# Moving half a gate's projection ahead of the attention output's projections, and respreading the work behind them

## The chip, the cores and the metric

The kernel runs on one core of a Trainium2 chip. The metric is the device time of one execution in microseconds (us); smaller is better. Every engine of the core (TensorE for products, VectorE, ScalarE and GpSimd for elementwise work, SyncE for issuing DMAs) runs its own list of instructions in order and waits for others through semaphores. The order within each list is fixed when the program is built: a planner goes through the program in its written order, estimates when each instruction's operands and buffers are ready, and gives an engine that is free the earliest-written instruction that is ready by that estimate.

## The reference

One encoder block over 512 tokens of width 1024, in float32:

```
z  = rmsnorm(x) @ W_in                 # a_q a_k a_v a_z, b_q b_k b_v, i_q i_k i_w, gate_a, gate_b
oA = gated_delta_rule(conv(a_q, a_k, a_v), ...) * silu(a_z)      # chunks of 64 tokens, 8 heads
oB = attention(rope(b_q), rope(b_k), b_v; 128 keys per query chosen by the indexer i_q, i_k, i_w)
x  = x + (sigmoid(gate_a) * (oA @ W_a) + sigmoid(gate_b) * (oB @ W_b)) @ W_out
x  = x + moe(rmsnorm(x))               # 16 experts, two per token
```

The delta rule solves, for each chunk and head, a unit lower triangular system of 64 x 64. The kernel inverts its diagonal blocks of 32 x 32 and combines them by products.

## The kernel before

**Pieces of weights.** A float32 product is done as three products of a high and a low half. The weights arrive in pieces of 256 rows by up to 512 columns, listed in `plan` by `want(key, ...)`. For each piece SyncE loads `raw` (three buffers), ScalarE copies the high half `whi`, and VectorE or GpSimd subtracts to get the low half `wlo` (two buffers each); the last argument of `want` names the engine of the low half. TensorE then runs 24 products on a piece. `tok_gen` and `feat_gen` are generators that yield after each piece; what stands between two yields is written behind the piece. A projection holds four accumulation banks and evacuates them after its last piece. Three more banks, `pm`, serve everything else.

**Order of the projections before:** "kv", "iq", "bq", "qk0", "v", "qk1", "gb0", "gb1" (the second gate), then "pb" (the attention output by W_b, two chunks of two pieces), "ga0", "z", "ga1" (the first gate in two halves, with "z" between), then the solve and "pa". "ga" is spilled to memory by `gate_spill` (four DMAs of 256 KB for each half).

**Behind the pieces.** `behind_projections()` yields once for each of the 24 pieces of "bq", "qk0", "v", "qk1", "gb0", "gb1" and takes that many steps of three generators: `PICKS` of `choose()` (the indexer's scores and the 128 largest of each row, 62 steps, VectorE's `max` and `match_replace`), `LOOKS` of `attention()` (53 steps), `NORMS` of `norms`. What is left over is drained behind "gb0" (choice) and "gb1" (attention). The query tiles of indexer and attention share the tag `tokq` with four buffers.

**The delta rule's systems.** `pre(g)`, for each of two groups of heads, has two steps for each of four token tiles: the first makes the system's matrices `ke` (products `pg`, `pkk`; exponentials; four products on VectorE) and writes the diagonal blocks to memory (`lane_n`, four DMAs); the second transposes keys and values and scales them (`r`, `kd` on VectorE, `qd` and a mask over `ke` on GpSimd). `pre(0)` runs behind the pieces of "pb", `pre(1)` behind three pieces of "ga0". `lanes()` then loads all diagonal blocks with one block on each partition (`LN`) and inverts them by a recurrence of 31 multiplies and 31 reductions on VectorE, each needing the one before. Its result `X` goes to memory (`lane_x`) and comes back as `TT`, with which `solve` begins. "z" and "ga1" are TensorE's work beside the recurrence.

Of the kernel before, what the change touches and what calls it, by code (L numbers as in the profile page):

```python
# [7 lines left out]
F32 = mybir.dt.float32  # L8
# [10 lines left out]
T = 4  # L19
# [12 lines left out]
LOWS_A = "DDDPDDPD"  # L32
PICKS = (0, 1, 5, 4, 5, 6, 0, 6, 4, 4, 5, 3, 5, 0, 4, 5, 4, 3, 2, 7, 0, 0, 0, 0)
LOOKS = (0, 0, 0, 0, 0, 0, 0, 0, 1, 2, 0, 4, 1, 2, 6, 3, 7, 2, 5, 6, 4, 6, 6, 0)
NORMS = (0, 0, 0, 0, 0, 0, 0, 0, 0, 1, 1, 1, 1, 1, 1, 0, 0, 2, 1, 1, 1, 1, 2, 2)
# [64 lines left out]
def body(tc, x, positions, norm1_g, w_in, w_proj_a, w_proj_b, w_out, norm2_g,  # L100
# [130 lines left out]
    for hf in range(2):  # L231
        want(f"gb{hf}", win, 8, [(GATE_B + 512 * hf, 512)], *low(LOWS[24 + 4 * hf:28 + 4 * hf]))
    for hf in range(2):
        want(f"pb{hf}", w_proj_b[0], 4, [(512 * hf, 512)], DVE)
    want("ga0", win, 8, [(GATE_A, 512)], *low(LOWS_A[:4]))
    want("z", win, 8, [(A_Z, 456)], POOL)
    want("ga1", win, 8, [(GATE_A + 512, 512)], *low(LOWS_A[4:]))
# [267 lines left out]
    def ev_iq(t, acc):  # L505
        q = AT_([128, 8, 64], name=f"iq{t}", tag="tokq", bufs=4)
# [137 lines left out]
    def ev_w3(t, acc):  # L644
        q = AT_([128, 8, 64], name=f"bq{t}", tag="tokq", bufs=4)
# [181 lines left out]
    for _ in gate_gen(1):  # L827
        tick(bg)
# [40 lines left out]
    def pre(g):  # L869

        Q = groups[g]
        hs = slice(4 * g, 4 * g + 4)
        Q.gl = []
        for t in range(T):
# [4 lines left out]
            eg = GP([128, 2, 128], name="eg", tag="eg", bufs=2)  # L879
# [22 lines left out]
            for b in range(4):  # L902
                SP.dma_start(lanes_of(lane_n, t, g, b), ke[32 * b:32 * b + 32, :, 0, 32 * b:32 * b + 32])
            yield
            ps = bank()
# [11 lines left out]
            Q.gl.append(gl)  # L917
            yield

    def lanes():  # L920

        LN = Ft([L, 32, 32], F32, "LN", "v0")
        SP.dma_start(LN, lane_n)
        X = Ft([L, 32, 32], F32, "X", "v1")
        POOL.memset(X, 0.0)
        POOL.memset(X.rearrange("p a b -> p (a b)")[:, ::33], 1.0)
        tmp = Ft([L, 1024], F32, "ltmp", "kq3")
# [7 lines left out]
        for d in range(1, 32):  # L935
# [3 lines left out]
            DVE.tensor_reduce(skew(flat[0], d, n, 1, 1), tv, axis=AX.X, op=OP.add)  # L939
# [144 lines left out]
    def z_chunk():  # L1084
        def ev(t, acc):
# [7 lines left out]
            zv = z.rearrange("p (h d) -> p h d", h=8)  # L1093
            POOL.tensor_tensor(zv, zv, angh[:, None, :].to_broadcast([128, 8, 64]), op=OP.mult)
# [13 lines left out]
    pre0, pre1 = pre(0), pre(1)  # L1108
    for hf in range(2):
        for _ in proj_b(hf):  # L1110
            tick([(pre0, 2)])
    drain(pre0)
    rk1 = [Ft([128, 2, 1024], F32, f"rk1{i}", ("obh", "obl")[i]) for i in range(2)]
    place(1, [ke_[1][:, t] for t in range(T)], [rk1[t // 2][:, t % 2] for t in range(T)])
    ga0 = gate_spill(0)
    for _ in range(3):
        tick([(ga0, 1), (pre1, 3)])
    drain(pre1)
    for t in range(2):
        clear_TT(t)  # L1120
    X = lanes()
# [670 lines left out]
```

## Time and profile before

| | |
|---|---|
| time, median of 3 runs | 724.35 us (723.95 to 725.03) |
| profiled execution: time, span | 722.27 us, 720.1 us |
| TensorE products, busy | 660.6 us (92%) |
| VectorE, busy | 531.5 us (74%) |
| ScalarE, busy | 412.9 us (57%) |
| GpSimd, busy | 258.9 us (36%) |
| chain that ended last | TensorE 61%, VectorE 22%, GpSimd 5% |

The span is the time between the profiled execution's first and last instruction; its own time is 2.2 us longer. Products are pipelined: a product's row shows some 0.39 us while the next one starts 0.23 us later, so TensorE's pace is read from starts, not from lengths.

### The profile page before, as it was taken

Reading aid. Unit: us, or ns where it says so; the run is one execution under the profiler, and the core shown is the slowest. Engines: PE = TensorE matmul, PEld = TensorE weight load, DVE = VectorE, ACT = ScalarE, POOL = GpSimd, SP = SyncE. Lnnn points to the kernel's source line nnn. Section 1 sums busy time; section 2 is a strip of 40 time slices with the busy share of each in tenths; the row PEclk is TensorE's granted clock in tenths of the full one; section 3 lists DMA queues with packets and bytes.
Section 4 is the critical chain, followed back from the end, with each engine's and each line's share of the span. In section 5 each row is a group of like instructions: output and inputs, shape, how many; then the busy total and the mean of one; then the engine's idle time right before and its main releaser. Section 6 shows DMA issues by size and latency. Waiting matters only on the chain.

```text
span 720.1 us, 10544 instructions
## 1 busy us (share of the span) xinstructions
PE 660.6 (92%) x3460; PEld 539.8 (75%) x3460; DVE 531.5 (74%) x1130; ACT 412.9 (57%) x736; POOL 258.9 (36%) x268
## 2 busy tenths in 40 slices
PE   3999977889889999999879999899999999999991
PEld 3888756666666777778768998878897888888871
DVE  4572689999995565642994566766678999999885
ACT  5443464586969764343323332344256998999863
POOL 3226716536341222345263111571142342334113
PEclk9999988999999999999999999999999999999996
DMA  7433213113130212325326200979779999999963
GB/s 264 114 108 88 86 30 89 58 31 87 30 88 5 84 58 63 74 57 148 88 76 182 94 2 1 348 235 355 257 235 311 352 294 287 300 276 274 289 213 119
DMA packets 84025, 110.76 MB, mean 154 GB/s; under 512 B 17435, under 2 KB 57883, under 8 KB 83840
## 3 DMA queue, kind: packets, MB, share of 16 engines
q1 hardware_dynamic: 79360, 101.70, 44.2%
q0 software_dynamic: 4320, 7.77, 4.4%
q8 instruction: 28, 0.46, 0.3%
q10 hardware_dynamic: 288, 0.59, 0.2%
q14 instruction: 29, 0.24, 0.1%
HBM read 101.22 MB, written 16.78 MB: 164 GB/s over the span
## 4 chain that ended last, share of the span: by engine, by line
PE 61%; DVE 22%; POOL 5%; issue 4%; DMA 4%; ACT 3%; SPq 0%; POOLq 0%; DVEq 0%; ACTq 0%
PE acc L130 47%; PE pm L130 5%; DVE xh L447 4%; DVE sn L595 3%; DVE ltmp L938 3%; DVE m L594 3%; DVE sn L585 2%; PE pm L1528 2%; POOL wlo L155 1%; DVE X L939 1%; POOL mTl L1209 1%; DMA x<-in_x_dram 1%; PE po L130 1%; ACT whi L154 1%; DMA xe<-h2d,ids 1%
## 5 line engine op out<-in xcount | busy, mean ns | idle before, releaser
L154 ACT ACTIVATE whi<-raw 128x1024 fp32r<-128x1024 f32 (+1 forms) x123 | 127.0, 1049 | 106.2 <-PE acc L130 83.5
L155 DVE TENSOR_TENSOR wlo<-raw,whi 128x1024 fp32r<-128x1024 f32 (+1 forms) x88 | 110.5, 1282 | 36.3 <-ACT whi L154 29.5
L155 POOL TENSOR_TENSOR wlo<-raw,whi 128x1024 fp32r<-128x1024 f32 (+1 forms) x35 | 89.0, 2542 | 124.0 <-ACT whi L154 107.0
L130 PE MATMUL acc<-hTh,whi 128*128 128x512 f32 x224 | 91.9, 410 | 5.1 <-ACT xh L445 4.2
L130 PE MATMUL acc<-hTh,wlo 128*128 128x512 f32 x224 | 90.4, 404 | 6.0 <-DVE wlo L155 5.9
L130 PE MATMUL acc<-whi,xhl 128*128 128x512 f32 x256 | 91.3, 410 | 0.3 <-DVE xhl L1535 0.3
L130 PE MATMUL acc<-hTl,whi 128*128 128x512 f32 x224 | 90.3, 403 | 0.0
L130 PEld LDWEIGHTS acc<-hTh,whi 128*128 128x128 f32 x224 | 43.7, 195 | 18.2 <-ACT xh L445 5.0
L130 PEld LDWEIGHTS acc<-hTh,wlo 128*128 128x128 f32 x224 | 43.5, 194 | 16.6 <-DVE wlo L155 7.3
L130 PEld LDWEIGHTS acc<-whi,xhl 128*128 128x128 f32 x256 | 48.1, 188 | 10.1 <-DVE xhl L1535 0.8
L130 PEld LDWEIGHTS acc<-hTl,whi 128*128 128x128 f32 x224 | 43.5, 194 | 10.1 <-issue 1.7
L130 PE MATMUL acc<-wlo,xhl 128*128 128x512 f32 x128 | 50.4, 394 | 0.0
L130 PE MATMUL acc<-whi,hTh 128*128 128x456 f32 (+1 forms) x120 | 46.1, 388 | 0.0
L1573 POOL DMA_INDIRECT accd<-yb,ids x14 | 23.9, 1704 | 58.7 <-ACT ah L154 58.7
L130 PE MATMUL acc<-wlo,hTh 128*128 128x456 f32 (+1 forms) x120 | 44.9, 374 | 0.0
L130 PE MATMUL acc<-whi,hTl 128*128 128x456 f32 (+1 forms) x120 | 44.7, 372 | 0.0
L1372 POOL DMA_INDIRECT xe<-h2d,ids x15 | 22.5, 1498 | 42.4 <-PE pm L1528 35.7
L447 DVE SCALAR_TENSOR_TENSOR xh<-xrb,sm,xh 128x511 f32<-128x511 f32 (+2 forms) x36 | 30.2, 891 | 0.0
L130 PE MATMUL acc<-whi,mTh 128*128 128x512 f32 (+1 forms) x72 | 27.4, 380 | 1.1 <-DVE ma L1203 1.1
L594 DVE MAX8 m<-sn 128x8 f32<-128x256 f32 (+2 forms) x48 | 26.6, 557 | 2.1 <-POOL sn L587 1.4
L130 PEld LDWEIGHTS acc<-wlo,xhl 128*128 128x128 f32 x128 | 24.2, 189 | 3.7
L938 DVE TENSOR_TENSOR ltmp<-X,LN 128x31 f32<-128x31 f32 (+15 forms) x31 | 20.5, 661 | 8.3 <-DMA LN<-lane_n 7.4
(466 smaller groups left out, 1662.4 us busy)
## 6 DMA issues: line engine op xcount, KB each, us to landing
raw<-in_w_in_dram SPq DMA_DIRECT2D x24, 512.0 KB, 3.6
raw<-in_w_exp_gate_dram SPq DMA_DIRECT2D x42, 256.0 KB, 8.2
raw<-in_w_exp_up_dram SPq DMA_DIRECT2D x42, 256.0 KB, 7.9
raw<-in_w_exp_down_dram SPq DMA_DIRECT2D x21, 512.0 KB, 9.5
raw<-in_w_in_dram SPq DMA_DIRECT2D x16, 256.0 KB, 3.2
raw<-in_w_out_dram SPq DMA_DIRECT2D x8, 512.0 KB, 9.1
raw<-in_w_in_dram SPq DMA_DIRECT2D x8, 456.0 KB, 3.5
x<-in_x_dram SPq DMA_DIRECT2D x4, 512.0 KB, 7.0
```

The costliest lines, as they stand in the source:

```text
L130: return ins_of(PE.matmul(o, l, r, start=start, stop=stop, skip_group_check=True))
L154: h = ins_of(ACT.activation(hi, src, AF.Copy))
L155: return h, ins_of((lo_eng or DVE).tensor_tensor(lo, src, f32(hi), op=OP.subtract))
L447: DVE.scalar_tensor_tensor(xh[:, j:], xr[:, :512 - j], cw[:, blk, 3 - j:4 - j], xh[:, j:], op0=OP.mult, op1=OP.add)
L585: DVE.scalar_tensor_tensor(s, r[:, :N], iwn[:, h:h + 1], s, op0=OP.mult, op1=OP.add)
L594: DVE.max(m8, sn[t])
L595: DVE.match_replace(out=sn[t], in_to_replace=m8, in_values=sn[t], imm_value=-2 * BIG)
L938: DVE.tensor_tensor(tv, skew(flat[0], 0, n, d, 1), skew(flat[1], d, n, d, 32), op=OP.mult)
L939: DVE.tensor_reduce(skew(flat[0], d, n, 1, 1), tv, axis=AX.X, op=OP.add)
L1372: return ins_of(POOL.indirect_dma_start(out=xe, out_offset=None, in_=h2d[0:128 * tiles], in_offset=bass.IndirectOffsetOnAxis(ap=idc, axis= ...
L1528: PE.transpose(ps[:, d * 128:(d + 1) * 128], xe[:, k * 128:(k + 1) * 128], C("ident"))
L1573: return ins_of(POOL.indirect_dma_start(out=accd, out_offset=bass.IndirectOffsetOnAxis(ap=idc, axis=0), in_=y, in_offset=None, bounds_chec ...
```

## The change

- "ga0" is projected and spilled directly after "gb1", ahead of "pb". Choice, attention and norms are spread over 28 pieces ("bq" to "ga0") by new tuples, and attention is drained behind "ga0".
- `pre(g)` is split into `systems(g)` (matrices and `lane_n`) and `sides(g)` (transposes and scales). Behind each of the four pieces of "pb" goes one step of `systems` of both groups; behind each piece of "z" one step of `sides` of both groups.
- `lanes()` is written behind "z"; `LN`, `X` and a smaller scratch have tiles of their own. Only "ga1" is written behind it.
- The low halves of "ga0", "z" and "ga1" are all VectorE's (before: GpSimd had one of "ga0", all of "z", one of "ga1").
- The four multiplications of `z` by the norm's gain on GpSimd are queued behind the recurrence's last instruction.
- `tokq` has six buffers instead of four.

```
-LOWS_A = "DDDPDDPD"
-PICKS = (0, 1, 5, 4, 5, 6, 0, 6, 4, 4, 5, 3, 5, 0, 4, 5, 4, 3, 2, 7, 0, 0, 0, 0)
-LOOKS = (0, 0, 0, 0, 0, 0, 0, 0, 1, 2, 0, 4, 1, 2, 6, 3, 7, 2, 5, 6, 4, 6, 6, 0)
-NORMS = (0, 0, 0, 0, 0, 0, 0, 0, 0, 1, 1, 1, 1, 1, 1, 0, 0, 2, 1, 1, 1, 1, 2, 2)
+PICKS = (0, 2, 3, 4, 4, 4, 3, 3, 3, 3, 3, 3, 3, 3, 3, 3, 3, 3, 3, 3, 3, 0, 0, 0, 0, 0, 0, 0)
+LOOKS = (0, 0, 0, 0, 0, 0, 0, 0, 0, 0, 1, 1, 1, 1, 2, 2, 3, 3, 3, 3, 3, 5, 5, 5, 5, 5, 5, 5)
+NORMS = (0, 0, 0, 0, 0, 0, 0, 0, 0, 1, 1, 1, 1, 1, 1, 0, 0, 2, 1, 1, 1, 1, 2, 2, 0, 0, 0, 0)
...
+    want("ga0", win, 8, [(GATE_A, 512)], DVE)
     for hf in range(2):
         want(f"pb{hf}", w_proj_b[0], 4, [(512 * hf, 512)], DVE)
-    want("ga0", win, 8, [(GATE_A, 512)], *low(LOWS_A[:4]))
-    want("z", win, 8, [(A_Z, 456)], POOL)
-    want("ga1", win, 8, [(GATE_A + 512, 512)], *low(LOWS_A[4:]))
+    want("z", win, 8, [(A_Z, 456)], DVE)
+    want("ga1", win, 8, [(GATE_A + 512, 512)], DVE)
...
-        q = AT_([128, 8, 64], name=f"iq{t}", tag="tokq", bufs=4)
+        q = AT_([128, 8, 64], name=f"iq{t}", tag="tokq", bufs=6)
...
-    for _ in gate_gen(1):
-        tick(bg)
+    for gate in (gate_gen(1), gate_spill(0)):
+        for _ in gate:
+            tick(bg)
     drain(att, nrm[1])
...
-    def pre(g):
+    def systems(g):
...
-            eg = GP([128, 2, 128], name="eg", tag="eg", bufs=2)
+            eg = GP([128, 2, 128], name=f"eg{g}{t}")
...
             for b in range(4):
                 SP.dma_start(lanes_of(lane_n, t, g, b), ke[32 * b:32 * b + 32, :, 0, 32 * b:32 * b + 32])
-            yield
+            Q.gl.append(gl)
+            Q.eg.append(eg)
+            yield
+
+    def sides(g):
+
+        Q = groups[g]
+        hs = slice(4 * g, 4 * g + 4)
+        for t in range(T):
+            ke, eg = Q.ke[t], Q.eg[t]
             ps = bank()
             for p in range(2):
                 PE.transpose(ps[:, p * 128:(p + 1) * 128], kq[2 * g + p][:, t, 0, :], C("ident"))
...
     def lanes():
 
-        LN = Ft([L, 32, 32], F32, "LN", "v0")
+        LN = GP([L, 32, 32], name="LN")
         SP.dma_start(LN, lane_n)
-        X = Ft([L, 32, 32], F32, "X", "v1")
+        X = GP([L, 32, 32], name="X")
...
-        tmp = Ft([L, 1024], F32, "ltmp", "kq3")
+        tmp = GP([L, 256], name="ltmp")
...
-            zv = z.rearrange("p (h d) -> p h d", h=8)
-            POOL.tensor_tensor(zv, zv, angh[:, None, :].to_broadcast([128, 8, 64]), op=OP.mult)
...
-    pre0, pre1 = pre(0), pre(1)
+    groups[1].ke = [ke_[1][:, t] for t in range(T)]
+    sys_ = [systems(g) for g in range(2)]
     for hf in range(2):
         for _ in proj_b(hf):
-            tick([(pre0, 2)])
-    drain(pre0)
+            tick([(sys_[0], 1), (sys_[1], 1)])
+    drain(*sys_)
     rk1 = [Ft([128, 2, 1024], F32, f"rk1{i}", ("obh", "obl")[i]) for i in range(2)]
     place(1, [ke_[1][:, t] for t in range(T)], [rk1[t // 2][:, t % 2] for t in range(T)])
-    ga0 = gate_spill(0)
-    for _ in range(3):
-        tick([(ga0, 1), (pre1, 3)])
-    drain(pre1)
+    side = [sides(g) for g in range(2)]
+    for _ in z_chunk():
+        tick([(side[0], 1), (side[1], 1)])
+    drain(*side)
     for t in range(2):
         clear_TT(t)
     X = lanes()
+    with after_(state["lanes"]):
+        for t in range(T):
+            zv = zt[t].rearrange("p (h d) -> p h d", h=8)
+            POOL.tensor_tensor(zv, zv, angh[:, None, :].to_broadcast([128, 8, 64]), op=OP.mult)
     ga1 = gate_spill(1)
-    drain(ga0, z_chunk())
     for _ in range(3):
         tick([(ga1, 1)])
     SP.dma_start(lane_x, X)
```

## Rows read from the trace of the kernel before

**Rows 1.** Stretches: length, busy PE, PEld, DVE, ACT, POOL, granted clock, DMA.
```profile
78.00:220.00 142.00, 122.06 (x528) 91.34 (x528) 134.39 (x310) 91.90 (x179) 65.34 (x54) 0.95 0.21 60
220.00:271.00 51.00, 50.60 (x240) 37.22 (x239) 27.53 (x71) 40.09 (x81) 11.51 (x13) 1.00 0.16 52
...
357.00:388.00 31.00, 24.96 (x103) 19.56 (x102) 24.41 (x41) 8.34 (x11) 16.87 (x20) 0.94 0.31 91
```

**Rows 2.** Timeline of VectorE (start, length, instruction): the selection's last instruction.
```profile
218.65 0.42 DVE L597 TENSOR_SCALAR sn<-sn 128x512 f32<-128x512 f32 x1
```

**Rows 3.** TensorE's waits, 78 to 219 us (total, times, longest).
```profile
PE acc L130 <- ACT xh L445: 4.2, 1, 4.2
```

**Rows 4.** Timeline of TensorE near 99 us.
```profile
99.76 0.79 PE L130 MATMUL acc<-hTh,whi 128*128 128x512 f32 x1 [0.70 <-ACT zb L647]
```

**Rows 5.** Timeline of TensorE: first products of "pb", "ga0", "z", "ga1" and two pieces of "ga1".
```profile
271.09 0.50 PE L130 MATMUL acc<-obh,whi 128*128 128x512 f32 x1
...
303.10 0.39 PE L130 MATMUL acc<-hTh,whi 128*128 128x512 f32 x1
...
337.16 0.36 PE L130 MATMUL acc<-whi,hTh 128*128 128x456 f32 x1
...
357.18 0.40 PE L130 MATMUL acc<-hTh,whi 128*128 128x512 f32 x1
...
376.22 0.39 PE L130 MATMUL acc<-hTh,whi 128*128 128x512 f32 x1
...
381.66 0.39 PE L130 MATMUL acc<-hTh,whi 128*128 128x512 f32 x1
```

**Rows 6.** Timeline: first products of three steps of `pre`, and the recurrence's first multiply.
```profile
309.09 0.56 PE L130 MATMUL pg<-GT,pick 128*128 128x128 f32 x4
...
313.29 0.56 PE L130 MATMUL pg<-GT,pick 128*128 128x128 f32 x4
...
329.14 0.56 PE L130 MATMUL pg<-GT,pick 128*128 128x128 f32 x4
...
341.81 0.22 DVE L938 TENSOR_TENSOR ltmp<-X,LN 128x31 f32<-128x31 f32 x1 [7.44 <-DMA LN<-lane_n]
```

**Rows 7.** Timeline of GpSimd and VectorE during the recurrence.
```profile
343.43 2.33 POOL L155 TENSOR_TENSOR wlo<-raw,whi 128x912 fp32r<-128x912 f32 x1 [2.09 <-ACT whi L154]
...
344.07 1.95 DVE L938 TENSOR_TENSOR ltmp<-X,LN 128x135 f32<-128x135 f32 x1
...
360.11 1.22 DVE L155 TENSOR_TENSOR wlo<-raw,whi 128x1024 fp32r<-128x1024 f32 x1
...
367.56 1.86 DVE L155 TENSOR_TENSOR wlo<-raw,whi 128x1024 fp32r<-128x1024 f32 x1
...
381.12 1.22 DVE L155 TENSOR_TENSOR wlo<-raw,whi 128x1024 fp32r<-128x1024 f32 x1
```

**Rows 8.** VectorE's groups, 271 to 388 us (busy us, mean ns, idle before).
```profile
L938 DVE TENSOR_TENSOR ltmp<-X,LN 128x31 f32<-128x31 f32 (+15 forms) x31 | 20.5, 661 | 8.3 <-DMA LN<-lane_n 7.4
...
L1092 DVE SCALAR_TENSOR_TENSOR zt<-zg,zt 128x512 f32<-128x512 f32 x4 | 4.4, 1102 | 0.0
...
L913 DVE TENSOR_TENSOR rk<-pm,scv 128x256 f32<-128x256 f32 x8 | 3.3, 411 | 0.0
```

**Rows 9.** GpSimd's groups, 271 to 388 us.
```profile
L916 POOL TENSOR_TENSOR ke<-ke,cst 128x512 f32<-128x512 f32 x8 | 10.3, 1288 | 21.0 <-DMA lane_n<-ke 21.0
...
L915 POOL TENSOR_TENSOR rk<-kq,eg 128x128 f32<-128x128 f32 x16 | 7.1, 461 | 0.0
...
L1094 POOL TENSOR_TENSOR zt<-zt,angh 128x512 f32<-128x512 f32 x4 | 5.8, 1457 | 14.1 <-DVE zt L1092 14.1
```

**Rows 10.** Timeline of SyncE and TensorE at the recurrence's end.
```profile
381.22 0.34 SPq L1126 DMA_DIRECT2D lane_x<-X  x1
...
387.52 1.05 PE L130 MATMUL pm<-rk,TT 128*128 128x128 f32 x8
```

**Rows 11.** Busy time in a stretch behind TensorE's idle time, with the granted clock.
```profile
369.90:373.30 3.40, 3.40 (x10) 2.62 (x9) 3.28 (x6) 0.00 (x0) 2.71 (x4) 0.50 0.55 154
```

More of the change, by code (lines that the diff above doesn't have):

```diff
@@ L644, in ev_w3 @@
     def ev_w3(t, acc):
-        q = AT_([128, 8, 64], name=f"bq{t}", tag="tokq", bufs=4)
+        q = AT_([128, 8, 64], name=f"bq{t}", tag="tokq", bufs=6)
         ACT.activation(q[:, 0:6, :], acc[:, 72:456].rearrange("p (h d) -> p h d", d=64), AF.Copy)
@@ L867, in lanes_of @@
         return d.rearrange("(t g h b) j i -> t g b j h i", t=T, g=2, h=4)[t, g, b]
-    def pre(g):
+    def systems(g):
         Q = groups[g]
-        hs = slice(4 * g, 4 * g + 4)
-        Q.gl = []
+        Q.gl, Q.eg = [], []
         for t in range(T):
@@ L916, in pre @@
             POOL.tensor_tensor(ke[:, :, 0, :], ke[:, :, 0, :], C("moff")[:, None, :].to_broadcast([128, 4, 128]), op=OP.mult)
-            Q.gl.append(gl)
             yield
     def lanes():
-        LN = Ft([L, 32, 32], F32, "LN", "v0")
+        LN = GP([L, 32, 32], name="LN")
         SP.dma_start(LN, lane_n)
-        X = Ft([L, 32, 32], F32, "X", "v1")
+        X = GP([L, 32, 32], name="X")
         POOL.memset(X, 0.0)
         POOL.memset(X.rearrange("p a b -> p (a b)")[:, ::33], 1.0)
-        tmp = Ft([L, 1024], F32, "ltmp", "kq3")
+        tmp = GP([L, 256], name="ltmp")
         flat = [v.rearrange("p a b -> p (a b)") for v in (X, LN)]
@@ L938, in lanes @@
             DVE.tensor_tensor(tv, skew(flat[0], 0, n, d, 1), skew(flat[1], d, n, d, 32), op=OP.mult)
-            DVE.tensor_reduce(skew(flat[0], d, n, 1, 1), tv, axis=AX.X, op=OP.add)
+            last = DVE.tensor_reduce(skew(flat[0], d, n, 1, 1), tv, axis=AX.X, op=OP.add)
+        state["lanes"] = ins_of(last)
         return X
```

## The prediction, made before the result was known

> **What bounds the kernel now.** I read the table of stretches first. From 78 to 220 us VectorE is busy 134.4 us of 142 while TensorE is busy 122.1, so TensorE stands still for 20 us; from 220 to 271 us TensorE is busy 50.6 of 51 and VectorE 27.5 [rows 1]. The selection's last instruction runs at 218.65 us, where the first stretch ends [rows 2]. Up to there choice and attention are held by VectorE, behind it by TensorE. The view of TensorE's waits shows how the lack comes through, 4.2 us at once where a chunk's banks wait for the convolution's copies, whose buffers VectorE empties [rows 3]; and at 99.76 us a product that waits for `zb`, a copy of the "bq" evacuation, which was late because its four `tokq` buffers were held by `iq` tiles [rows 4]. From 271 to 357 us TensorE hardly stops. Then comes the second bound: the recurrence of `lanes()` runs on VectorE from 341.81 to 381.2 us [rows 6, 7], TensorE has 25.0 busy us in the last 31 [rows 1], and the first product that uses the result starts at 387.52 [rows 10], right behind the last piece of "ga1", which begins at 381.66 [rows 5] and is 5.4 long. There both chains end together. So I price two stretches: 78 us to the end of attention (271.09), and from there to 387.5.
>
> **Choice and attention.** One piece of 512 columns takes TensorE 5.44 us (376.22 to 381.66) [rows 5]; "ga0" moved ahead is 4 x 5.44 = 21.8 us. Had nothing else changed, the projections "pb" would start at 271.1 + 21.8 = 292.9 us. The new tuples take the selection's 62 steps to the 21st piece (before: the 18th), and 23 steps of attention have been asked for by then instead of 28. VectorE's work up to the selection's end is 134.4 us less five steps of attention. The stretch 220 to 271 has 25 of the 53 steps and 27.5 us of VectorE, so 1.1 us a step [rows 1]: 129 us. VectorE now idles 7.6 us there; I let it idle 8. The selection ends at 78 + 137 = 215 us. TensorE's work besides whole pieces was 122.1 - 15 x 5.44 = 40.5 us, five steps less (0.95 us each, below) make 36. In 137 us with 4 us of residual waiting fit (137 - 36 - 4) / 5.44 = 17.8 pieces instead of 15. Left are 6.2 of 24: 33.7 us, and 30 steps; before, five pieces (27.2) and 25 steps filled 51 us, so 23.8 / 25 = 0.95 us a step, 28.5 us. With 2 us of waiting the attention ends at 215 + 64 = 279 us: 13.8 us gained.
>
> The bounds: all 20 idle us gone gives 273; none gone gives 293. I take a value near the middle since both engines would now be over 90% busy in one stretch, each in a fixed order, and ScalarE is busy 40.1 of 51 us where I pack 30 steps over six pieces [rows 1].
>
> The `tokq` buffers (4 to 6) cost nothing; they remove the wait at 99.76, which is within the 20 us. The gate's four spills and four weight loads move with it; the DMA share is 0.16 to 0.21 there [rows 1]. One low half of "ga0" goes from GpSimd to VectorE, 1.22 us [rows 7], in a stretch where VectorE has room.
>
> **The projections with the systems.** Before, four pieces and four whole steps of `pre` took 271.09 to 303.10, 32.0 us, so a step costs 32.0/4 - 5.44 = 2.56 us of TensorE [rows 5]. Now two `systems` steps follow each piece. Their transposes are gone to `sides`, yet a second step waits for the three banks; I take the full 2 x 2.56 = 5.1. Call T the end of the last piece: T = 279 + 21.8 + 3 x 5.1 = 316 us. SyncE issues two sets of four `lane_n` writes per 10.5 us. TensorE then still has one pair (5.1), four "z" pieces (337.16 to 357.18: 20.0 us [rows 5]), the `sides` transposes (at most 8 x 0.5) and "ga1" (21.8): it is through at T + 51 = 367 us.
>
> **When the recurrence starts.** It needs the last system in memory. Before, the last step's first product was at 329.14 and the recurrence began at 341.81: 12.7 us [rows 6]. The second of two steps in a row started 4.2 us behind the first (309.09, 313.29 [rows 6]). So it starts at T + 16.9 = 333 us. Against the start of "z" that is some 15 us, where before it was 4.6. The load of `LN` no longer waits for `v0`, `v1` and `kq3`, but it didn't wait for them before either: its row is released by the DMA.
>
> **How long it runs.** 39.4 us before: two low halves inside (1.22, 1.86 [rows 7]), four `zt` products (4.4), 31.9 of its own (its multiplies' mean is 0.66 us [rows 8]). Of these, four multiplies ran 1.4 to 2.2 us where their neighbours take 0.5; one of them starts at 344.07, during a GpSimd subtraction that began at 343.43, and ends with it at 346.0 [rows 7]. That is 5.5 us of blocking, and 26.4 are left. After: 26.4; all four low halves of "ga1" fall inside, 4 x 1.22 = 4.9; `zt` 4.4; the last two pairs of `sides`, 12 instructions, about 4 us by a mean of 0.41 [rows 8]; and blocking by GpSimd. Four `sides` steps of 1.29 + 2 x 0.46 us [rows 9] run beside it, 8.8 us at most; the angle products (four) and the low halves on GpSimd are gone from this stretch. Between 0 and 8.8 I take 3, as 5.5 us came from some 14 us of such work before. Sum 42.7: the recurrence ends at 376 us.
>
> The Trainium skill ("SBUF — State Buffer", Who interferes with whom) says that a VectorE instruction with two inputs in SBUF and a GpSimd instruction that reads SBUF exclude each other for the whole instruction. The row at 344.07 agrees (1.95 us, ending with the subtraction). Taken at every overlap, this rule speaks against the change: the third rival.
>
> **Behind it.** From the end of the recurrence (write at 381.22) to the first product 387.52 is 6.3 us [rows 10]: the first product starts at 376 + 6.3 = 382 us. TensorE has been through since 367 and idles 15 us. In the kernel before, an idle of 6 us of TensorE in this place was followed by a stretch of 3.4 us at a granted clock of 0.50 [rows 11], the 1.2 GHz level; I add 1.7 us. The angle products (4 x 1.46 on GpSimd [rows 9]) now follow the recurrence; `outputs` uses `zt` only some 20 us later, so they cost nothing unless they block VectorE. The later stages are unchanged and shift as a whole. So: attention -13.8, the stretch behind it 103.1 us against 94.6 (116.4 less "ga0") +8.5, clock +1.7: -3.6 us. The profiled execution (720.1 us of span, 722.27 us) becomes 718.7; it lies 2.1 us below the median of the runs, so for the median 720.7 us.
>
> **The rivals.**
> 1. The recurrence stays covered. If the planner puts the low halves and `zt` behind or ahead of it and nothing blocks it, it ends at 333 + 26.4 = 359.4, the first product comes at 367 with TensorE's own work, 15 us sooner, no clock loss: 704 us. Against it: both kinds of instruction cut into it before. Chance 0.15.
> 2. The choice doesn't spread: slower. VectorE was saturated for 142 us, and its work is hardly less; if it starves while TensorE's fixed order makes it wait, or ScalarE holds the last 30 steps, the attention ends at 289 instead of 279: 730.7 us. It decides from 282.7 us on (gain under 10.2 us), as the stretch behind loses that. Chance 0.20.
> 3. GpSimd's work blocks in full: 8.8 us instead of 3, and the angle products take another 1 us from VectorE at the start of the solve: 727.5 us. Chance 0.12. The skill's rule named above would give this, and one overlap bears it out.
> 4. Two low halves of "ga1" fall behind the recurrence (one did before, at 381.12 [rows 7]): then TensorE's last pieces end 1.2 + 2 x 5.44 = 12.1 us after it instead of 6.3: 726.5 us. Chance 0.08.
>
> **The numbers.** The forecast has 0.45; its own range is 713 to 728. The range 707 to 732 leaves out most of the first rival and the tail of the second. A measurement of this kernel can tell about 0.2% (1.45 us) from no change. The forecast gives 0.32 faster, 0.08 same, 0.05 slower; the first rival 0.15 faster; the second 0.02, 0.02, 0.16; the third and fourth 0.02, 0.04, 0.14. Sum: 0.51, 0.14, 0.35.
>
> **What would show it.** In the profile after: "pb" starting near 279 us; TensorE idle between 78 us and there well under 20; the selection's last instruction near 215; the recurrence starting near 333 and taking about 43; TensorE idle before the first product of the solve by some 15 us. If "pb" starts after 283 the second rival has it; if no idle stands before the solve, the first. The prediction is wrong if the stretch from the start of "pb" to the solve is not near 103 us, or if later stages change in length.

## The result, and the profile after

The changed kernel takes 730.38 us (median of 7 runs, 726.98 to 731.18), the kernel before 724.35 (7 runs by now, 720.44 to 726.84): a ratio of 1.0077 (95%: 1.0057 to 1.0097), slower. The forecast was 720.7 and faster. The profiled execution of the changed kernel takes 731.18 us, its span is 729.4 us. In the rows PE is TensorE (PEld its weight loads), DVE VectorE, ACT ScalarE, POOL GpSimd and SP SyncE.

The stretches, from 78 us to the selection's end, from there to the first product of "pb", and from "ga1" to just behind the start of the solve (columns as in [rows 1]):

```profile
78.00:217.50 139.50, 123.36 (x521) 91.76 (x519) 130.62 (x285) 83.08 (x164) 60.54 (x53) 0.94 0.23 65
217.50:288.70 71.20, 70.05 (x342) 55.37 (x341) 41.32 (x101) 51.39 (x102) 10.07 (x13) 1.00 0.22 67
351.80:394.60 42.80, 24.04 (x107) 19.57 (x105) 32.42 (x60) 8.30 (x10) 14.48 (x22) 0.83 0.43 137
```

Up to the selection's end TensorE is idle for 139.5 - 123.36 = 16.1 us (before about 20, [rows 1]); behind it, it is full for 71 us. In the third line it has 24 busy us of 43 at a mean granted clock of 0.83. These are the two places where the time went, and the timeline shows them: the selection's last instruction on VectorE, then TensorE's first products of "pb", "z", "ga1", the last piece of "ga1" and the solve (answering to [rows 2, 5, 10]).

```profile
217.58 0.43 DVE L596 TENSOR_SCALAR sn<-sn 128x512 f32<-128x512 f32 x1
...
288.68 0.50 PE L129 MATMUL acc<-obh,whi 128*128 128x512 f32 x1
325.95 0.36 PE L129 MATMUL acc<-whi,hTh 128*128 128x456 f32 x1
351.78 0.48 PE L129 MATMUL acc<-hTh,whi 128*128 128x512 f32 x1
370.06 0.39 PE L129 MATMUL acc<-hTh,whi 128*128 128x512 f32 x1
392.89 0.55 PE L129 MATMUL pm<-rk,TT 128*128 128x128 f32 x1 [17.23 <-DMA TT<-lane_x]
```

"pb" starts at 288.68 us: that is 17.6 later than before, where "ga0" alone is worth 21.8, so the whole spreading gave 4.2 us. From "pb" to the solve it is 104.2 us; before it was 116.4 with "ga0", 94.6 without. The last row names the price: TensorE waits 17.23 us for the recurrence's result. The recurrence's first multiply and the write of its result (answering to [rows 6, 10]):

```profile
338.53 0.22 DVE L945 TENSOR_TENSOR ltmp<-X,LN 128x31 f32<-128x31 f32 x1 [1.34 <-DMA LN<-lane_n]
...
385.70 0.32 SPq L1136 DMA_DIRECT2D lane_x<-X  x1
```

and what VectorE does in between, by groups (busy us, mean ns, idle before):

```profile
L945 DVE TENSOR_TENSOR ltmp<-X,LN 128x31 f32<-128x31 f32 (+15 forms) x31 | 17.1, 552 | 2.2 <-DMA LN<-lane_n 1.3
L946 DVE TENSOR_REDUCE X<-ltmp 128x31 f32<-128x31 f32 (+30 forms) x31 | 10.5, 338 | 1.0
L154 DVE TENSOR_TENSOR wlo<-raw,whi 128x1024 fp32r<-128x1024 f32 (+1 forms) x6 | 7.6, 1261 | 0.0
L1100 DVE SCALAR_TENSOR_TENSOR zt<-zg,zt 128x512 f32<-128x512 f32 x4 | 5.0, 1242 | 0.0
L919 DVE TENSOR_TENSOR rk<-pm,eG 128x256 f32<-128x256 f32 x6 | 2.5, 418 | 0.4 <-PE pm L916 0.4
L920 DVE TENSOR_TENSOR rk<-pm,kds 128x256 f32<-128x256 f32 x6 | 2.5, 416 | 0.0
L921 DVE TENSOR_TENSOR rk<-pm,scv 128x256 f32<-128x256 f32 x6 | 2.5, 414 | 0.0
```

VectorE is full: 27.6 us of the recurrence's own, and 20.1 us of other work standing between its steps in VectorE's list (rows overlap a little, so they add up to more than the 47.1 us from the first multiply to the last reduction's end). The clock behind TensorE's idle time (answering to [rows 11]):

```profile
380.20:397.30 17.10, 4.41 (x21) 4.44 (x22) 5.06 (x15) 1.19 (x2) 0.76 (x2) 0.50 0.55 161
```

The granted clock stands at 0.50, the 1.2 GHz level, for 17.1 us, so the solve begins at that level; from its first product to that of the projection behind it there are 62.3 us instead of 60.6.

The sum of the profiled pair: 17.6 - 12.2 (104.2 against 116.4) + 1.7 = 7.1 us. The spans differ by 9.3; the other 2.2 us come later: from the first output product to the first of the experts, the routing, it is 70.9 us against 67.7, and the experts take 1.0 us less. In the kernels below the routing takes between 64.7 and 71.0 us whatever the edit, so I don't count it to the change. The medians differ by 6.0 us.

### The profile page after: what moved, and what is told of

It is laid out like the page before. It is cut to its first block, busy times and chain, and to the rows that moved or that the text cites. A ratio compares the mean times of both kernels' runs of the same rounds, so it can differ in the third digit from the quotient of the medians.

```text
span 729.4 us, 10510 instructions
## 1 busy us (share of the span) xinstructions
PE 662.0 (91%) x3460; PEld 545.0 (75%) x3460; DVE 538.9 (74%) x1136; ACT 409.3 (56%) x734; POOL 237.4 (33%) x262
## 4 chain that ended last, share of the span: by engine, by line
PE 62%; DVE 20%; ACT 5%; DMA 5%; issue 4%; POOL 3%; SPq 0%; POOLq 0%; ACTq 0%; DVEq 0%
PE acc L129 47%; PE pm L129 6%; DVE xh L446 3%; DVE sn L594 3%; DVE m L593 2%; DVE ltmp L945 2%; DVE wlo L154 2%; PE pm L1538 2%; PE po L129 1%; DMA raw<-in_w_exp_down_dram 1%; DVE X L946 1%; ACT whi L153 1%; POOL mTl L1219 1%; DMA x<-in_x_dram 1%; PE pkk L129 1%
## 5 line engine op out<-in xcount | busy, mean ns | idle before, releaser
L154 DVE TENSOR_TENSOR wlo<-raw,whi 128x1024 fp32r<-128x1024 f32 (+1 forms) x94 | 116.4, 1263 | 25.0 <-ACT whi L153 24.8
L154 POOL TENSOR_TENSOR wlo<-raw,whi 128x1024 fp32r<-128x1024 f32 (+1 forms) x29 | 71.7, 2473 | 121.1 <-ACT whi L153 101.8
L129 PEld LDWEIGHTS acc<-hTh,whi 128*128 128x128 f32 x224 | 43.4, 194 | 17.5 <-issue 4.3
L129 PEld LDWEIGHTS acc<-hTh,wlo 128*128 128x128 f32 x224 | 43.4, 194 | 11.1 <-DVE wlo L154 1.9
L129 PE MATMUL acc<-whi,mTl 128*128 128x512 f32 (+1 forms) x72 | 26.5, 368 | 0.0
```

The costliest lines, as they stand in the source:

```text
L129: return ins_of(PE.matmul(o, l, r, start=start, stop=stop, skip_group_check=True))
L154: return h, ins_of((lo_eng or DVE).tensor_tensor(lo, src, f32(hi), op=OP.subtract))
```

## The experiments

Each table row has the ratio to the kernel before on the same chip, then three readings of the profiled execution: us from the first product of "qk0" to the first of "pb"; TensorE's idle us from that first product to the selection's end (length less its busy time, as above); us from "pb" to the solve's first product. Without interval: one run.

| kernel | us | ratio (95%) | qk0 to pb | idle | pb to solve |
|---|---|---|---|---|---|
| before | 724.35 | | 192.6 | 19.9 | 116.4 |
| changed | 730.38 | 1.0077 (1.0057 to 1.0097) | 210.5 | 16.1 | 104.2 |
| b_cover | 717.42 | 0.9925 (0.9903 to 0.9947) | 193.6 | 19.4 | 112.6 |
| a_alone | 736.82 | 1.0191 (1.0159 to 1.0224) | 210.3 | 15.7 | 110.5 |
| short_rec | 709.10 | | 210.2 | 15.7 | 86.7 |
| low_gps | 732.99 | 1.0143 (1.0110 to 1.0177) | 211.2 | 16.0 | 106.9 |
| half_sel | 731.62 | | 211.9 | 14.8 | 104.3 |
| conv_third | 724.24 | | 202.0 | 11.1 | 104.6 |
| half_both | 718.73 | | 199.0 | 7.1 | 104.9 |
| spread24 | 729.09 | 1.0089 (1.0062 to 1.0116) | 207.8 | 16.3 | 108.2 |
| late_looks | 733.20 | 1.0096 (1.0059 to 1.0132) | 213.1 | 15.2 | 105.5 |
| tokq_only | 725.14 | 0.9994 (0.9971 to 1.0018) | 191.8 | 16.8 | 117.5 |
| conv_spread | 725.23 | 1.0018 (0.9996 to 1.0040) | 207.4 | 15.6 | 105.2 |
| conv_spread2 | 725.27 | 1.0006 (0.9989 to 1.0023) | 206.0 | 14.6 | 104.4 |
| slot_only | 727.66 | 1.0035 (1.0010 to 1.0059) | 208.3 | 14.6 | 104.1 |
| b_cover2 | 719.99 | 0.9923 (0.9894 to 0.9953) | 191.8 | 16.8 | 113.5 |
| b_conv | 723.38 | 1.0003 (0.9980 to 1.0026) | 197.6 | 19.1 | 112.6 |
| b_slot | 712.69 | 0.9833 (0.9810 to 0.9856) | 187.3 | 15.3 | 112.6 |

**The two parts of the change apart.** "b_cover" keeps the split of the systems, and puts "ga0" back, with the tuples and the four buffers of the kernel before:

```
-    for _ in z_chunk():
+    for _ in gate_spill(0):
         tick([(side[0], 1), (side[1], 1)])
...
     X = lanes()
+    drain(z_chunk())
```

> The second part of the change alone: "ga0" stands between "pb" and "z" again, choice and attention over 24 pieces with the tuples and four tokq buffers of the kernel before; systems of both groups behind "pb", sides behind "ga0" instead of "z", lanes() behind them, "z" and "ga1" after it. Theory A (the loss is the cover that "ga0" took away from the recurrence; the split of the systems itself is good): "pb" starts at 271, "ga0" at 308, the recurrence runs from 321 to about 368, TensorE works through to 376 and the first product of the solve comes at 376 to 379 instead of 387.5 in the kernel before: 713 to 717 us, 8 to 11 below the kernel before. Theory B (the split of the systems costs as much as it gives, through GpSimd and VectorE): 722 us or more.

"a_alone" moves "ga0" and spreads the tuples, with `pre` and `lanes()` as before (its edit is shown against the kernel before):

```
-    ga0 = gate_spill(0)
+    zc = z_chunk()
     for _ in range(3):
-        tick([(ga0, 1), (pre1, 3)])
+        tick([(zc, 1), (pre1, 3)])
```

> The first part of the change alone: "ga0" ahead of "pb", the tuples over 28 pieces, six tokq buffers; pre(0) stands behind "pb" as before, pre(1) behind three pieces of "z" (before: of "ga0"), lanes() as before behind that, so only "ga1" covers the recurrence. Theory A (the move takes the cover away, the split of the systems gave part of it back): "pb" at 288.7, the recurrence starts at 354 to 360 and ends at 392 to 398, the solve starts at 398 to 405 instead of 392.9; 735 to 743 us, 5 to 12 above the changed kernel. Theory B (the split of the systems is worth nothing here, since VectorE is the bound beside the recurrence anyway): the solve starts at 390 to 395, 728 to 732 us.

Both theories A held in direction. The split alone is 0.75% faster, the move alone 1.9% slower; the change, which has both, is 0.8% slower. In "b_cover" TensorE's waits from 272 to 384.6 us are these:

```profile
PE acc L129 <- DVE wlo L154: 3.2, 2, 2.6
PE pg L129 <- ACT eg L880: 0.3, 1, 0.3
```

and its timeline has the write of the recurrence's result and the first solve product:

```profile
366.01 0.34 SPq L1136 DMA_DIRECT2D lane_x<-X  x1
...
384.71 0.38 PE L129 MATMUL pm<-rk,TT 128*128 128x128 f32 x2
```

Nothing waits for `TT`; 3.8 us of idle time are left. The solve came 6 to 9 us later than I expected (384.7 against 376 to 379): TensorE's own work now sets it, and "ga1" took 27.2 us (357.5 to 384.7) instead of 21.8, with the 3.2 us of waits and, behind them, 3.4 us at a granted clock of 0.50. In "a_alone" the other half shows in TensorE's waits, 290 to 405 us:

```profile
PE pm L130 <- DMA TT<-lane_x: 16.7, 1, 16.7
PE acc L130 <- DVE wlo L155: 4.4, 1, 4.4
PE pg L130 <- ACT eg L883: 0.9, 3, 0.3
```

**What sets the start of the solve.** "short_rec" leaves out every second step of the recurrence:

```
-        for d in range(1, 32):
+        for d in range(1, 32, 2):
```

> The changed kernel with the even diagonals of the recurrence left out (16 of its 31 multiplies and reductions are left). The recurrence ends at 385.7 us in the changed kernel, its own instructions take 27.6 us of 47.1. Theory A (the recurrence alone sets the start of the solve, and TensorE's 17 idle us there are its price): it ends near 372, the first product of the solve comes at 379 to 381 instead of 392.9, the stretch at granted clock 0.5 behind it is gone or shorter than 7 us, and the span falls by 12 to 16 us, from 729.4 to 713 to 717. Theory B (the pieces of "ga1", whose low halves wait on VectorE, set it): TensorE's last piece still ends at 375 and the solve starts no sooner than 385.

The recurrence ends at 369.8 us, and the wait is gone: the first solve product follows the last of "ga1" at once, 17.5 us sooner against "pb" than in the changed kernel (timeline of TensorE).

```profile
376.57 0.39 PE L129 MATMUL acc<-hTh,wlo 128*128 128x512 f32 x1
376.80 0.38 PE L129 MATMUL pm<-rk,TT 128*128 128x128 f32 x2
```

The stretch around it has the full granted clock:

```profile
370.00:390.00 20.00, 19.80 (x141) 17.41 (x140) 6.38 (x13) 8.87 (x15) 4.57 (x8) 1.00 0.74 206
```

From the solve to the projection behind it there are 60.7 us, as before: the 1.7 us more of the changed kernel come with the idle time. (Its span falls by 22.2 us in all, more than expected; 6.1 of these are the routing, 64.8 us here, which varies with no edit.) "low_gps" gives low halves back to GpSimd:

```
-    want("z", win, 8, [(A_Z, 456)], DVE)
-    want("ga1", win, 8, [(GATE_A + 512, 512)], DVE)
+    want("z", win, 8, [(A_Z, 456)], POOL)
+    want("ga1", win, 8, [(GATE_A + 512, 512)], DVE, DVE, POOL, DVE)
```

> The changed kernel with the low halves of "z" (four) and of the third piece of "ga1" on GpSimd as in the kernel before, instead of VectorE. Beside the recurrence (47.1 us) VectorE runs 7.6 us of low halves, 7.5 us of sides, 5.0 us of zt products and 27.6 us of its own. Theory A (these instructions add up, in order): two to three low halves fewer there, the recurrence takes 43 to 45 us, the solve starts 2 to 4 us sooner against "pb" (104.2 us now). Theory B (each GpSimd subtraction of 2.2 to 2.9 us holds a multiply of the recurrence until it ends, as at 372.26 us, where a multiply took 2.27 us): the recurrence takes 46 us or more, and the solve does not come sooner.

The recurrence took 44.1 us, as theory A has it, and yet the solve came 2.7 us later against "pb", where A had it sooner, and B had no gain because of a longer recurrence. The recurrence began later, 53.8 us behind "pb" instead of 49.9. SyncE's timeline tells why:

```profile
329.97 4.56 SPq L902 DMA_DIRECT2D lane_n<-ke  x8
337.73 0.39 SPq L288 DMA_DIRECT2D raw<-in_w_in_dram  x1
338.36 0.34 SPq L930 DMA_DIRECT2D LN<-lane_n  x1
```

The load `LN` stands behind a load of weights whose buffer comes free only when the low half of "z" on GpSimd (335.54 to 337.70) has read it. In the changed kernel `LN` directly follows the `lane_n` writes. So that part of the change, low halves on VectorE, was worth 2.7 us between "pb" and the solve, by a way that I had not priced.

**What holds choice and attention.** "half_sel" takes work from VectorE, evenly; "conv_third" takes it from the convolution; "half_both" does both:

```
         for i in range(TOPK // 8):
+            if i % 2:
                 DVE.max(m8, sn[t])
                 DVE.match_replace(...)
...
-        for j in (1, 2, 3):
+        for j in (1,):
             DVE.scalar_tensor_tensor(xh[:, j:], xr[:, :512 - j], ...)
```

> The changed kernel with every second of the selection's 48 rounds of max and match_replace left out (so 64 of each row's 128 largest are found); order and all else as they are. In the changed kernel a round takes VectorE 0.56 + 0.54 + 0.09 us, so 24 rounds are 28.5 us. Theory A (VectorE's amount of work holds choice and attention up to the selection's end, TensorE has 193.4 busy us from 78 us to the start of "pb" and 17 idle): the idle time mostly goes, "pb" starts at 272 to 277 us instead of 288.7. Theory B (the fixed order and the waits for banks and ScalarE hold it, not VectorE's amount): the idle stays above 10 us, "pb" starts at 282 us or later.

> The changed kernel with two of the three tap products of each convolution left out (24 VectorE instructions of 0.89 us less between 78 and 218 us, 20 us in all); order and all else as they are. Halving the selection moved nothing, although it took 21 us from VectorE. Theory A (not the amount counts but bursts: VectorE's list holds runs of up to nine convolution products, 8.2 us, and small instructions that free a bank or make an operand stand behind them): the waits of TensorE for rel, mx and iqs fall, its idle goes from 17 to under 10 us, "pb" starts at 276 to 282 us. Theory B (the idle comes from the hand-offs themselves, each step's product waiting for the one before to go through ScalarE and VectorE): the idle stays above 13, "pb" starts at 285 to 291.

> The changed kernel with every second round of the selection and two of three convolution products left out together (VectorE some 43 us lighter than in the changed kernel between the first "qk0" product and "pb", 172 us there). Theory A (amount: VectorE has to fall well below TensorE's load before the idle goes): idle before the selection's end under 5 us, "pb" under 198 us behind the first "qk0" product (210.5 in the changed kernel, 202.0 without the convolution products alone). Theory B (the order within the lists and the hand-offs make the idle, of which the convolution's are one part): idle 8 to 12 us, 200 to 204 us.

Half the selection gone moved nothing: in a stretch of the same length VectorE is 21 us less busy and TensorE does the same work ("half_sel", 80 to 219.5 us):

```profile
80.00:219.50 139.50, 123.24 (x521) 92.12 (x519) 109.55 (x214) 83.59 (x166) 59.81 (x53) 0.94 0.23 65
```

With a third of the convolution's products, and as much taken from VectorE, TensorE does 4.6 us more in a stretch of that length ("conv_third", 79 to 218.5 us):

```profile
79.00:218.50 139.50, 127.86 (x559) 96.18 (x558) 111.83 (x272) 88.16 (x174) 62.95 (x56) 0.98 0.24 69
```

TensorE's waits in "half_sel":

```profile
PE pm L129 <- ACT rel L580: 5.6, 3, 3.7
PE pm L129 <- DVE mx L668: 4.9, 2, 3.1
PE pm L129 <- DVE iqs L528: 2.6, 1, 2.6
PE acc L129 <- ACT xh L444: 1.5, 1, 1.5
```

They are of the same kinds as in the changed kernel (78 to 217.6 us, answering to [rows 3]; a wait for `zb`, as in [rows 4], is no longer among them):

```profile
PE pm L129 <- DVE mx L667: 5.9, 3, 2.9
PE pm L129 <- DVE iqs L528: 4.0, 2, 2.7
PE pm L129 <- ACT rel L580: 2.2, 2, 2.0
PE ssq L129 <- ACT sq L620: 2.0, 1, 2.0
PE acc L129 <- ACT xh L444: 1.9, 2, 1.7
```

So VectorE's amount of work is not what TensorE waits for. The convolution's products matter more: with 24 of 36 gone "pb" comes 8.5 us sooner, as theory A has it (281.1 us), with a little more idle time than it had. With both gone it is 11.5; half the selection is worth 3 us once the convolution is light, so the amount counts a little then. Even so TensorE idles 7.1 us before the selection's end; 199.0 and 7.1 lie between what the two theories of "half_both" expected. (A lighter selection ends sooner, so the table's idle time covers less there. Up to "pb" TensorE idles 17.3 us in the changed kernel, 17.5 in "half_sel", 12.6 in "conv_third" and 9.8 in "half_both".) The timeline of the changed kernel near 140 us shows how the convolution does it (VectorE, ScalarE, TensorE):

```profile
140.16 8.79 DVE L446 SCALAR_TENSOR_TENSOR xh<-xrb,sm,xh 128x510 f32<-128x510 f32 x10
...
146.39 0.63 ACT L451 ACTIVATE vT<-xh 128x512 f32<-128x512 f32 x1 [2.38 <-DVE xh L446]
146.93 0.61 ACT L620 ACTIVATE sq<-kq 128x512 f32<-128x512 f32 x1
...
147.60 1.87 PE L129 MATMUL ssq<-sq,cst 128*8 128x512 f32 x2 [2.02 <-ACT sq L620]
...
148.87 0.47 DVE L582 TENSOR_SCALAR sn<-rel,iwn 128x512 f32<-128x512 f32 x1
...
149.38 0.60 ACT L580 ACTIVATE rel<-pm 128x512 f32<-128x512 f32 x1 [0.31 <-DVE sn L582]
```

Ten products of one chunk stand in a row in VectorE's list. ScalarE's silu of that chunk (`vT`) waits for one of them, the squares `sq` of another chunk stand behind it in ScalarE's list, and TensorE waits 2.02 us for the squares. The scores `sn` come on VectorE only at 148.87, so the next score is copied out of its bank only at 149.38. In the same way the low half of `iqs` at 95.52 stands behind three rounds of the selection, though ScalarE had made its high half by 92.44, and TensorE waits 2.69 us for it. The Trainium skill ("PSUM — Partial Sum Buffer", Engine vs sequencer instructions) says that the queues of ScalarE and VectorE are strictly first in, first out; these rows agree.

Next, the same work placed otherwise. "spread24" stretches the choice, "late_looks" puts attention off, "tokq_only" gives the kernel before the two buffers:

```
spread24
-PICKS = (0, 2, 3, 4, 4, 4, 3, 3, 3, 3, 3, 3, 3, 3, 3, 3, 3, 3, 3, 3, 3, 0, 0, 0, 0, 0, 0, 0)
-LOOKS = (0, 0, 0, 0, 0, 0, 0, 0, 0, 0, 1, 1, 1, 1, 2, 2, 3, 3, 3, 3, 3, 5, 5, 5, 5, 5, 5, 5)
+PICKS = (0, 2, 3, 4, 4, 4, 3, 3, 3, 3, 3, 3, 3, 3, 3, 3, 2, 2, 2, 2, 2, 2, 2, 1, 0, 0, 0, 0)
+LOOKS = (0, 0, 0, 0, 0, 0, 0, 0, 0, 0, 1, 1, 1, 1, 2, 2, 3, 3, 3, 3, 3, 3, 3, 4, 5, 5, 5, 5)
...
     for _ in gate_gen(0):
         tick(bg)
-    drain(sel)
...
+    drain(sel)
     drain(att, nrm[1])
late_looks
+LOOKS = (0, 0, 0, 0, 0, 0, 0, 0, 0, 0, 0, 0, 0, 0, 0, 0, 0, 0, 5, 5, 5, 5, 5, 5, 5, 6, 6, 6)
tokq_only (on the kernel before)
-tag="tokq", bufs=4
+tag="tokq", bufs=6
```

> The changed kernel with the selection's 62 steps spread over the first 24 of the 28 pieces instead of 20: the drain of the choice stands behind "gb1" instead of "gb0", the tuple of the choice ends (3, 3, 2, 2, 2, 2, 2, 2, 2, 1), that of the attention (3, 3, 3, 3, 3, 3, 3, 4, 5, 5, 5, 5). Theory A (the written order, which ends the choice at the 20th piece, makes TensorE wait for a VectorE that is full): with the choice thinner, TensorE's idle falls from 17 to under 8 us, "pb" starts at 279 to 283 instead of 288.7, and the time falls by 5 to 9 us against the changed kernel. Theory B (what VectorE, ScalarE and TensorE hand to each other costs the idle, however it is spread): "pb" starts at 287 to 291 and the time stays within 2 us of 730.4.

> The changed kernel with attention's 53 steps put off: none up to the 18th piece, then five or six behind each of the last ten (before the 20th piece 10 steps instead of 20). Theory A (attention's steps between the selection's steps cause TensorE's waits): the idle before the selection's end falls from 17 to under 10 us, and "pb" starts at 278 to 284 instead of 288.7, the time falls by 4 to 9 us against 730.4. Theory B (the idle is the choice's and the convolution's own, and attention packed more densely waits for ScalarE, which is busy 51 of the last 71 us already): "pb" starts at 288 or later, the time is 730 or more.

> The kernel before with six tokq buffers instead of four, nothing else. Theory A (the buffers are worth only what they are a condition for; the 0.7 us wait at 99.76 us goes, the wait of 4.2 us there was the convolution's): "pb" starts within 2 us of 271.1, the time within 0.2% of the kernel before. Theory B (the early waits of the kernel before, 4.3 to 4.6 us in each of the pieces at 88 and 115 us, are these buffers'): "pb" starts at 264 to 268, the time falls by 3 to 7 us, and this is all that the first stretch of the change gained.

None of them brought TensorE's idle time under 15 us. "spread24" reached "pb" 2.8 us sooner and lost it again: attention's last output was made at 293.3 us, behind the start of "pb" at 286.2 (in the changed kernel at 287.0, ahead of it), and "pb" to solve took 108.2 us. (In its expectation the drain is said to stand behind "gb1"; it stood behind "ga0".) "late_looks" ended the selection 13 us sooner and took 87 us from there to "pb" instead of 71. The two buffers alone are worth nothing that can be measured.

**The convolution's place.** "conv_spread" writes the twelve products of a chunk three at a time behind four pieces. In it the k block's copy takes the q block's slot before the products have read it, so q and k get other values; "conv_spread2" mends that with the edit that "slot_only" makes alone:

```
conv_spread
+        def taps():
             for j in (1, 2, 3):
                 DVE.scalar_tensor_tensor(xh[:, j:], xr[:, :512 - j], ...)
+        held_taps.append((fb, taps, dst, xh, out))
...
         for i, n in enumerate(PICKS):
+            late_taps()
             tick([(sel, n), (att, LOOKS[i]), (nrm[i // 16], NORMS[i])])
slot_only, conv_spread2, b_slot
-        xr = xrb[:, blk % 4]
+        xr = xrb[:, fb]
```

> The changed kernel with the same convolution products on VectorE, but not written in bursts: the twelve products of a chunk, which stood together behind its last piece, are written three at a time behind that piece and the three pieces after it (the silu follows the last of them; the steps of norms move with it). Nothing is left out. Theory A (TensorE idles because small hand-off instructions stand behind bursts in VectorE's list): as with two thirds of the products left out, though with VectorE as busy as before, the idle before the selection's end goes from 16 to 9 to 12 us and "pb" stands 202 to 206 us behind the first "qk0" product instead of 210.5; the time falls by 4 to 8 us against the changed kernel. Theory B (what helped in that run was the 20 us less of VectorE's work): 209 to 212 us, no gain.

> The convolution's products spread over four pieces as in conv_spread, now with a slot of their own for each block's copy (in conv_spread the k block's copy took the place of the q block's before it was used). Theory A (bursts): "pb" 204 to 208 us behind the first "qk0" product as there (207.4), 724 to 727 us. Theory B (what conv_spread gained came from the dependency that it lost): 209 to 212 us, 729 to 732 us.

> The changed kernel, with the copies of the convolution's inputs in slot fb of the four instead of slot blk % 4, so that the q and k blocks of a chunk no longer share a slot; nothing else. Theory A (ScalarE's copies wait for VectorE's products on the shared slot and hold TensorE's banks: the waits of acc for xh, 1.9 us): "pb" 2 to 4 us sooner than 210.5 behind the first "qk0" product, 726 to 729 us. Theory B (the copies are not what comes last): 209.5 to 211.5, no change of the time beyond 2 us.

"conv_spread" fell between its theories: 207.4 us, with the idle time still at 15.6. With all work kept, the two edits bring "pb" 4.6 us sooner (206.0) and the time from 1.0077 to 1.0006 of the kernel before; the slots alone give 2.3 us and 1.0035. The slots were a chain that I had not seen: `blk % 4` gives the q and the k block of a head pair the same slot, so ScalarE's copy of the second waits for VectorE's products on the first. It is a row of ScalarE's waits, 78 to 289 us in the changed kernel, which "slot_only" and "b_slot" don't have (in "b_cover" it is 5.9 us):

```profile
ACT xrb L442 <- DVE xh L446: 4.0, 3, 3.3
```

The idle time fell only from 16.1 to 14.6 us in "conv_spread2"; the rest of the gain is the clock, with 10.2 us at a granted clock of 0.50 before "pb" instead of 17.0. TensorE's list then waits at another place ("conv_spread2", 78 to 218 us):

```profile
PE pm L129 <- DVE bqs L537: 7.5, 2, 5.7
PE pm L129 <- DVE iqs L537: 2.6, 1, 2.6
PE pm L129 <- ACT rel L589: 1.7, 2, 1.5
```

So bursts are part of the cause, not all of it.

**Towards a faster version.** "b_cover2" is "b_cover" with six buffers and one low half of "ga1" on GpSimd, "b_conv" with the products spread (and q and k altered as in "conv_spread"), "b_slot" with the unshared slots and six buffers:

> The second part alone (label b_cover, 717.4 us) with two edits: six tokq buffers, and the low half of the second piece of "ga1" on GpSimd, as in the kernel before. In b_cover TensorE waits 3.2 us for low halves of "ga1" that VectorE makes behind the recurrence, and is otherwise busy from 272 to the solve at 384.7. Theory A (that wait is the last one there): it goes, the solve starts 3 us sooner against "pb", the time is 713 to 716 us. Theory B (GpSimd's subtraction blocks the recurrence and the next low half is late instead): TensorE waits as much at another piece, 716 to 719 us.

> The second part alone (label b_cover) with the convolution's products spread in the same way over the 24 pieces, and six tokq buffers. In b_cover "pb" stands 193.6 us behind the first "qk0" product, with 19.4 idle us of TensorE before the selection's end. Theory A (bursts): 185 to 190 us, the time 5 to 9 us below b_cover, 709 to 713 us. Theory B (VectorE's amount, or tuples that fit the bursts): 191 to 195 us and 716 to 720 us.

> The second part alone (b_cover) with a slot for each block's copy and six tokq buffers. Theory A (the shared slots cost: the kernel before waits 4.2 us for xh at one place): "pb" 188 to 191 us behind the first "qk0" product instead of 193.6, the time 2 to 5 us below b_cover (0.985 to 0.990 of the kernel before). Theory B (the order only moves the idle elsewhere): 191 to 195 us and 0.990 to 0.994.

The low half on GpSimd gave nothing, as theory B has it: TensorE waits 3.5 us for that half instead. Spreading the products made "b_cover" slower: with the tuples of the kernel before, waits for `iqs` and `mx` (6.4 and 5.8 us) took the place of others. The slots and buffers gave 6.3 us up to "pb" (1.8 of them the buffers', going by "b_cover2") and the fastest kernel here that keeps all the work, 712.69 us, 1.7% under the kernel before. Its two stretches, up to the selection's end and from there to "pb":

```profile
78.50:215.10 136.60, 121.28 (x528) 91.36 (x527) 131.87 (x310) 93.72 (x182) 59.90 (x53) 0.95 0.22 62
215.10:265.80 50.70, 48.97 (x236) 36.71 (x234) 29.04 (x71) 36.77 (x75) 11.94 (x15) 1.00 0.17 52
```

Here too 136.6 - 121.3 = 15.3 us of idle time stay.

## Why the prediction was wrong

**The step that failed** is in "Choice and attention": "In 137 us with 4 us of residual waiting fit (137 - 36 - 4) / 5.44 = 17.8 pieces instead of 15." The selection's end came nearly as worked out (217.6 against 215), and so did TensorE's other work (123.4 - 16 x 5.44 = 36.3 us against 36). But the waiting was 16.1 us, not 4, and 16 pieces fitted. From there on 71.2 us were left where I had 64, and "pb" started at 288.68 instead of 279. Under it lay a reading of [rows 1] that the runs refute: that this stretch is "held by VectorE". VectorE was busy for 94% of it, but taking 21 us of it away changed nothing. A busy share near one told that VectorE has no room; it did not tell that TensorE waits for its amount. TensorE waits for single small instructions that stand behind others in an order fixed beforehand, and fewer steps of choice for each piece leave these places as they are. By the text's own test ("if "pb" starts after 283 the second rival has it") the second rival came true, in its number too (730.7), though not by the reason given first for it, a full VectorE. That its number was met so closely is in part luck: the spans differ by 9.3 us, the medians by 6.0.

**What was right.** "pb" to "z" took 37.3 us, against 37.1; but two errors cancel in it, since seven of the eight `systems` steps ran ahead of "z", not six, and a step cost TensorE 2.2 us, not 2.56 ((37.3 - 21.8) / 7). The first product behind the recurrence came 7.2 us after the write, against 6.3. TensorE idled 17 us there, against 15. The clock cost 1.7 us, as forecast.

**Where sizes were off.** The recurrence started 12.6 us behind the first product of "z", which follows "pb" (forecast 16.9), because the last `systems` step came early (327.35 us) and the recurrence followed it by 11.2 us, not 12.7, and took 47.1 us (42.7). Its parts, forecast and measured: own work with blocking 29.4 and 27.6; low halves 4.9 (four) and 7.6 (six, since the last of "z" and one of "pa" fell inside too); `zt` 4.4 and 5.0; `sides` 4.0 (12 instructions) and 7.5 (18). The two errors cancel, so nearly the whole miss up to the solve is the first stretch: 9.7 us at "pb", 9.7 at the recurrence's end, 10.9 at the solve. The 2.2 us behind it were not forecast either.

**The other rivals.** The first (covered recurrence) is out by the 17.23 us wait. For the third, GpSimd's blocking, the rows show both: one multiply is held until a GpSimd subtraction ends, while the one that started 0.03 us ahead of that subtraction is not (timeline of VectorE and GpSimd in the changed kernel).

```profile
371.14 0.63 DVE L945 TENSOR_TENSOR ltmp<-X,LN 128x252 f32<-128x252 f32 x1
371.17 2.87 POOL L154 TENSOR_TENSOR wlo<-raw,whi 128x1024 fp32r<-128x1024 f32 x1 [2.71 <-ACT whi L153]
...
372.26 2.27 DVE L945 TENSOR_TENSOR ltmp<-X,LN 128x247 f32<-128x247 f32 x1
```

The Trainium skill ("SBUF — State Buffer", Who interferes with whom) says that the port pair which VectorE and GpSimd share is an exclusive lock, and that issue order decides who blocks; these rows agree (371.17 + 2.87 = 374.04, the multiply ends at 374.53). So do the four `zt` products: two that started ahead of GpSimd's products took 0.69 us each, two that started during one took 1.79 and ended 0.55 us behind it, as here:

```profile
355.14 1.30 POOL L1132 TENSOR_TENSOR zt<-zt,angh 128x512 f32<-128x512 f32 x1
355.19 1.79 DVE L1100 SCALAR_TENSOR_TENSOR zt<-zg,zt 128x512 f32<-128x512 f32 x1
```

Estimated from the lengths of their neighbours, GpSimd held VectorE for 4.6 us beside the recurrence, 2.4 of them in two multiplies (1.25 and 2.27 us where others take 0.5 and 0.6) and 2.2 in `zt`. The third rival's 8.8 us did not come, nor a cost at the start of the solve. With fewer low halves on GpSimd the recurrence's own work was 27.6 us against 31.0 before (20.5 of multiplies [rows 8] and 10.5 of reductions), and in "low_gps" it was 30.1. The fourth rival did not show: the low halves of "ga1" ran inside the recurrence.

**An order that was no order.** I let the four products of `z` with the norm's gain (the prediction's "angle products") follow the recurrence. They ran at 350 to 358 us, beside it: the edge put no wait on GpSimd. The instruction that they were to follow is VectorE's, and the edge may order only instructions on one engine's list; no run tests that. They took GpSimd 5.9 us and held VectorE for 2.9 of the 4.6 us above (2.2 in `zt`, 0.7 in a multiply).

**What stays open.** Which instructions make up the last 15 us of idle time in choice and attention was seen in rows (in the changed kernel a few waits of 1 to 3 us each), not settled by an edit; only leaving work out took it under 14 us. Many of these waits are products into the three banks `pm` behind an instruction that empties a bank (`rel`, `mx`); whether another share of the banks would hide them was not tried. Why spread products help with the new tuples and hurt with the old ones was not tried further.

## What to carry to other kernels

A busy share of 94% doesn't make an engine the bound: before a gain from a lighter load is priced, look at what ends each wait of the engine that is to be filled, since it may be one small instruction behind a burst in a fixed list, or a scratch slot that two blocks need not share (worth 2.3 us in the changed kernel). Before filler work is moved ahead, price the chain that it covered: "ga0" stood between "pb" and "z", ahead of a 40 us recurrence; without it TensorE came to the solve 17 us before the recurrence's result, and the move could only be paid by idle time elsewhere, which the new order hardly filled (19.9 us before, 16.1 after). Starting the chain earlier with the filler left in place gave 0.75%, and with the slots 1.7%.

## What the runs showed that was not expected

In "low_gps" a slow consumer on GpSimd reached the recurrence through SyncE's list: the load of weights waits for its buffer, and `LN` waits behind it (3.2 us). Idle time in choice and attention costs more than its length: in the changed kernel TensorE waited 1.97 us up to 143.58 and 2.91 us up to 172.52, and the granted clock stood at 0.50 for 6.8 us from 144.66 and for 6.8 us from 171.97. With two thirds of the convolution's products left out, 6.8 us at that level were left of 17.0 before "pb", and TensorE's busy time there fell with it, from 193.2 to 189.4 us for the same products.
